# Two more up pairs of each layer, and the last single columns of gate and up, with two units in seven products

## The chip, the cores and the metric

The kernel runs on one core of one Trainium2 chip, in one launch. The metric is the time of one execution on the device in microseconds (us). A core has a TensorE (PE in the profile, with its weight loads as PEld), a VectorE (DVE), a ScalarE (ACT), a GpSimd (POOL) and a SyncE (SP). SP does no arithmetic here: it issues the transfers of the weights.

## The reference, cut to what matters

Two layers over x of 256 rows and 2048 columns, all in float32. The part that the change touches is the second half of each layer, the feed-forward block, whose hidden width is 5632:

```
h2 = rms_norm(x, ffn_norm[l])
x = x + (jax.nn.silu(h2 @ w_gate[l]) * (h2 @ w_up[l])) @ w_down[l]
```

The first half of a layer (a combined input projection, windowed attention, a spatial gating unit, sigmoid gates, an output projection) runs ahead of it with the same machinery and is left as it is.

## The kernel before, in words

**Three matmuls for one.** A float32 operand is split into a high part, rounded to the format fp32r that TensorE multiplies, and a low part, the remainder. ACT makes the high part of a weight block (`high`, line 258), DVE the low part (`low`, line 266), and `three` (lines 401 to 403) adds high x high, low x high and high x low into one PSUM bank. The 256 rows of activations (`Unit.hi` and `Unit.lo`) are the stationary operand, 128 by 128 at a time; 512 columns of weights are the moving one.

**Jobs, units, parts.** A *job* multiplies all rows by two blocks of 512 weight columns. It goes through the weights' rows in *units* of 512, four units for a matrix with 2048 rows. A unit's weights come in two transfers of 1 MB, 256 rows by 1024 columns each, into one of five buffers (`N_RAW`, line 34). Half a transfer, 256 rows by 512 columns, is a *part*. A unit that is taken *whole* has four parts; each is split once by ACT and DVE and used in 12 matmuls (two blocks of 128 rows, two of 128 in depth, three matmuls), 48 for the unit.

**Seven products.** The first `m` units of a job (`Job.m`, line 106) are multiplied by a scheme with seven block products in place of eight. With weight blocks 11, 12, 21, 22 (the first digit for the depth, the second for the columns) the products are called 11, t1, t2, 21, t3, 22 and t4; t1 to t4 take sums of weight blocks, which DVE makes (`add`, line 242, one instruction for each of the four), and sums of activations, which are made once when the activations are (`combine`, line 503). A product is a part of its own with a high and a low of its own and 6 matmuls, so the unit has 42 matmuls. Two corrections of accumulators by DVE (line 440) and some copies of them by ACT (lines 435 and 437) are made once in a job, whatever `m` is.

**The order is written out by hand.** The parts of all jobs form one list. With `m` = 2 a job starts with nine products in a row, and the last five stand between whole parts of its other units:

```
    HEAD = ("11a", "t1a", "t2a", "21a", "t3a"), ("11a", "11b", "t1a", "t1b", "t2a", "t2b", "21a", "t3a", "t3b")
    TAIL = (("22a",), ("t4a",)), (("22a",), ("22b", "21b"), ("t4a",), ("t4b",))
```

`Stream.fill` (line 270) lets ACT and DVE run ahead of TensorE by at most five parts (`N_LOW`, line 37) and issues the transfers as their buffers come free (`load`, line 199); the sums are due three to seven parts ahead of the job (`SUM_AT`, line 96). Each engine then works through its own instructions in order. Work that is neither a part nor a matmul (evictions, transpositions, splits of activations) is hung on *slots*: a whole part is one slot, a product half a slot (`tick`, line 334). How late some of it comes depends on whether the *next* job has `m` = 0, 1 or 2 (`behind`, line 311): the eviction of the job's last accumulator comes 1, 1.5 or 3 slots behind its end, the transposition of a finished block 2, 3 or 7 slots (lines 40 and 315).

**The feed-forward block.** Its 11 blocks of 512 hidden columns are taken in three rounds, (0 1 2 3), (4 5 6 7) and (8 9 10). A round goes through its columns in pairs: a gate job, whose results ACT evicts with the Silu (line 1090), and an up job, whose results DVE multiplies into them (line 1096). Blocks are then transposed by DVE and 16 small transfers from POOL's queue (`gathered`, line 481) and split again (lines 589 and 592, or 510 to 525 where sums are wanted). Block 10 stands alone: one job takes its gate columns and its up columns as the pair. Two down jobs end a round, one for each half of the output's columns; a round's first block of hidden rows goes in seven products there. What follows names a job by its first block: "up 4" multiplies the up columns of blocks 4 and 5, "gate/up 10" is the single one, "down 8" is the third round's first down job. Where `m` is set:

```
            for f in fs[::2]:
                if f + 1 < NF:
                    for w, m in ((w_gate, M_FFN[0] if f else 0), (w_up, M_FFN[1] if f in UP_TWO else 1)):
                        add_job([w[l, :, f * CW:(f + 2) * CW]], m=m)
                else:
                    add_job([w[l, :, f * CW:(f + 1) * CW] for w in (w_gate, w_up)], m=M_FFN[2])
```

(lines 177 to 182). In the kernel before, the jobs of a layer's feed-forward block have in their order: gate 0 with `m` = 0, up 0 with 2, gate 2 with 2, up 2 with 2, two downs with 1; gate 4 with 2, up 4 with 1, gate 6 with 2, up 6 with 2, two downs with 1; gate 8 with 2, up 8 with 1, gate/up 10 with 1, two downs (three units each) with 1.

Of the kernel before, what the change touches and what calls it, by code (L numbers as in the profile page):

```python
# [42 lines left out]
Q_STEP = 4  # L43
LOAD_BY = (1, 2, 3, 4)
ROUNDS = ((0, 1, 2, 3), (4, 5, 6, 7), (8, 9, 10))
M_OUT, M_FFN, M_DOWN = (0, 1), (2, 2, 1), ((1, 1), (1, 1), (1, 1))
UP_TWO = (0, 2, 6)
M_Q = 0
M_GATE, M_ATT, M_SGU = (1, 1, 1, 1), (0, 0), (1, 0)
M_V, M_U = 1, 1  # L50
# [4 lines left out]
def hybrid_trunk(ctx: ExitStack, tc: tile.TileContext, x, mix_norm, w_in, q_norm, k_norm, sinks,  # L55
# [106 lines left out]
    for l in range(DEPTH):  # L162
# [13 lines left out]
        for fs, ms in zip(ROUNDS, M_DOWN):  # L176
# [4 lines that stand above are left out]
# [970 lines left out]
```

## Time and profile before

| | |
|---|---|
| median of 3 runs | 2444.57 us (2441.78 to 2444.78) |
| the profiled execution | 2442.93 us, its span 2441.2 us |
| PE, DVE, ACT, POOL busy | 99%, 83%, 59%, 19% of the span |
| granted clock of TensorE | 0.999 |

The profile is of one execution. Its busy time counts an instruction from its start to its end; neighbouring matmuls overlap in the record, so their mean duration is longer than the step from one to the next. "Idle before, releaser" says how long an engine stood still before an instruction and which instruction ended the wait. In the view of windows a row is a stretch of time: its bounds and length, then the busy time of each engine with the number of instructions, the granted clock and the share of the transfer engines' time. The windows used here begin and end with the first matmul of a job, found by counting matmuls: a job has 48 for each whole unit and 42 for each in seven products. An instruction that overlaps the edge of a window is counted in it, so that 180 matmuls read as 181.

### The profile page before, as it was taken

How to read it: one execution, taken by the hardware profiler on the slowest of the kernel's cores; microseconds unless marked ns; L12 is line 12 of the kernel's file. 1: busy time of each engine (PE TensorE's matmuls, PEld its weight loads, DVE VectorE, ACT ScalarE, POOL GpSimd, SP SyncE). 2: the span in 40 equal slices, each digit the busy share in tenths (PEclk: the TensorE clock that was granted, in tenths of full speed). 3: DMA queues.
4: the chain of work that ended last, by engine and by line, in shares of the span. 5: the costliest groups of instructions: out<-in, count | busy, mean ns of one | idle time of the engine just before them, and what ended most of it. 6: DMA issues, size and time to landing. Idle time of an engine off the chain costs nothing. (4 is left out here: it accounts for less than half of the span.)

```text
span 2441.2 us, 30915 instructions
## 1 busy us (share of the span) xinstructions
PE 2428.7 (99%) x10926; PEld 2004.8 (82%) x10926; DVE 2015.1 (83%) x2213; ACT 1441.9 (59%) x1762; POOL 474.2 (19%) x903
## 2 busy tenths in 40 slices
PE   9999999999999999999999999999999999999999
PEld 7888888888788888888888888888888888888887
DVE  7898768787988798788879977687789887988786
ACT  6565546466655666465666655554667555755563
POOL 1421300531220022002235122014402200220020
PEclk9999999999999999999999999999999999999999
DMA  8555556776586757666776555566855766585764
GB/s 311 200 194 186 176 178 224 231 260 228 177 278 205 258 190 255 228 243 207 259 253 230 189 169 192 188 200 219 291 208 210 256 218 247 175 282 192 263 202 162
DMA packets 179053, 539.20 MB, mean 221 GB/s; under 512 B 23873, under 2 KB 26545, under 8 KB 178897
## 3 DMA queue, kind: packets, MB, share of 16 engines
q1 hardware_dynamic: 150832, 508.51, 60.6%
q0 software_dynamic: 27744, 28.44, 3.8%
q8 instruction: 85, 1.39, 0.2%
q14 instruction: 72, 0.58, 0.1%
q10 hardware_dynamic: 320, 0.27, 0.0%
HBM read 492.04 MB, written 16.78 MB: 208 GB/s over the span
## 5 line engine op out<-in xcount | busy, mean ns | idle before, releaser
L266 DVE TENSOR_TENSOR wlo<-raw,whi 128x1024 fp32r<-128x1024 f32 (+1 forms) x960 | 1153.6, 1218 | 339.8 <-PE acc L402 244.7
L258 ACT ACTIVATE whi<-raw 128x1024 fp32r<-128x1024 f32 (+1 forms) x960 | 1000.9, 1057 | 658.7 <-PE acc L403 567.5
L401 PE MATMUL acc<-whi,uh 128*128 128x512 f32 x2964 | 1160.2, 391 | 1.6 <-DVE gate L1061 1.5
L402 PE MATMUL acc<-wlo,uh 128*128 128x512 f32 x2964 | 1154.2, 389 | 2.6 <-DVE wlo L266 2.6
L403 PE MATMUL acc<-whi,ul 128*128 128x512 f32 x2964 | 1153.9, 389 | 0.2 <-DVE ul L550 0.2
L491 POOL DMA_DIRECT2D tt<-blk x800 | 393.4, 499 | 1655.7 <-DVE blk L485 714.4
L401 PEld LDWEIGHTS acc<-whi,uh 128*128 128x128 f32 x2964 | 556.4, 188 | 120.3 <-issue 2.3
L402 PEld LDWEIGHTS acc<-wlo,uh 128*128 128x128 f32 x2964 | 556.6, 188 | 118.7 <-DVE wlo L266 5.2
L403 PEld LDWEIGHTS acc<-whi,ul 128*128 128x128 f32 x2964 | 556.4, 188 | 117.1 <-DVE ul L550 0.6
L401 PE MATMUL acc<-whi,sh 128*128 128x512 f32 x496 | 193.4, 390 | 0.0
L402 PE MATMUL acc<-wlo,sh 128*128 128x512 f32 x496 | 193.2, 390 | 0.2 <-DVE wlo L266 0.2
L403 PE MATMUL acc<-whi,sl 128*128 128x512 f32 x496 | 193.1, 389 | 0.0
L258 ACT ACTIVATE whi<-sum 128x1024 fp32r<-128x1024 f32 x124 | 131.2, 1058 | 103.3 <-PE acc L403 95.6
L266 DVE TENSOR_TENSOR wlo<-sum,whi 128x1024 fp32r<-128x1024 f32 x124 | 150.4, 1217 | 4.2 <-PE acc L402 4.2
L401 PEld LDWEIGHTS acc<-whi,sh 128*128 128x128 f32 x496 | 93.1, 188 | 20.6 <-ACT acc L437 1.5
L402 PEld LDWEIGHTS acc<-wlo,sh 128*128 128x128 f32 x496 | 93.1, 188 | 20.0 <-DVE wlo L266 0.9
L403 PEld LDWEIGHTS acc<-whi,sl 128*128 128x128 f32 x496 | 93.1, 188 | 19.5
L437 ACT ACTIVATE acc<-acc 128x512 f32<-128x512 f32 x144 | 84.7, 588 | 25.3 <-PE acc L403 24.9
L242 DVE TENSOR_TENSOR raw<-raw,sum 128x1024 f32<-128x1024 f32 x62 | 75.9, 1225 | 2.1
L242 DVE TENSOR_TENSOR raw<-raw,raw 128x1024 f32<-128x1024 f32 x62 | 75.6, 1219 | 1.7 <-DMA raw<-in_w_gate_dram 1.7
L242 DVE TENSOR_TENSOR sum<-raw,raw 128x1024 f32<-128x1024 f32 x62 | 75.8, 1222 | 1.2
L242 DVE TENSOR_TENSOR sum<-raw 128x1024 f32<-128x1024 f32 x62 | 75.6, 1219 | 1.2 <-DMA raw<-in_w_gate_dram 1.2
(126 smaller groups left out, 1013.5 us busy)
## 6 DMA issues: line engine op xcount, KB each, us to landing
raw<-in_w_in_dram SPq DMA_DIRECT2D x112, 1024.0 KB, 5.4
raw<-in_w_down_dram SPq DMA_DIRECT2D x88, 1024.0 KB, 6.6
raw<-in_w_gate_dram SPq DMA_DIRECT2D x80, 1024.0 KB, 6.4
raw<-in_w_up_dram SPq DMA_DIRECT2D x80, 1024.0 KB, 6.5
raw<-in_w_out_dram SPq DMA_DIRECT2D x32, 1024.0 KB, 7.1
tt<-blk POOLq DMA_DIRECT2D x800, 32.0 KB, 4.8
raw<-in_w_attn_branch_dram SPq DMA_DIRECT2D x16, 1024.0 KB, 6.1
raw<-in_w_sgu_branch_dram SPq DMA_DIRECT2D x16, 1024.0 KB, 5.5
```

The lines of the kernel that those rows point to most:

```text
L242: nc.vector.tensor_tensor(out=self.raw(dst), in0=self.raw(one), in1=self.raw(two), op=ALU.subtract)
L258: nc.scalar.activation(hi[:, k, :], raw[:, k, :], AF.Copy)
L266: nc.vector.tensor_tensor(out=lo[:, k, :], in0=raw[:, k, :], in1=hi[:, k, :].bitcast(F32), op=ALU.subtract)
L401: nc.tensor.matmul(ps, a, hi, start=first, stop=False, skip_group_check=True)
L402: nc.tensor.matmul(ps, a, lo, start=False, stop=False, skip_group_check=True)
L403: nc.tensor.matmul(ps, b, hi, start=False, stop=last, skip_group_check=True)
L437: nc.scalar.activation({"11": x, "t2": e, "t3": y}[name], a, AF.Copy)
L491: nc.gpsimd.dma_start(blocks(d)[:, :, i] if whole else d[:, i].rearrange("p k t c -> p (k t) c"), src)
```

## The change

Two constants. `UP_TWO` lists the first blocks of those up pairs that have `m` = 2 (the others have 1); `M_FFN` holds `m` for the gate pairs, the up pairs in `UP_TWO`, and the single columns.

```diff
-M_OUT, M_FFN, M_DOWN = (0, 1), (2, 2, 1), ((1, 1), (1, 1), (1, 1))
-UP_TWO = (0, 2, 6)
+M_OUT, M_FFN, M_DOWN = (0, 1), (2, 2, 2), ((1, 1), (1, 1), (1, 1))
+UP_TWO = (0, 2, 4, 6, 8)
```

So in each of the two layers up 4, up 8 and gate/up 10 take two of their four units in seven products where they took one. Through `behind`, the jobs ahead of these three (gate 4, gate 8, up 8) hang their late work on later slots. The sums of the activations that a second unit needs are made already, for the jobs that had `m` = 2 before.

## Prediction

> **What bounds the kernel now.** I read the page first, then the waits, then the windows cut at the jobs of the feed-forward block.
>
> ```profile
> span 2441.2 us, 30915 instructions
> PE 2428.7 (99%) x10926; PEld 2004.8 (82%) x10926; DVE 2015.1 (83%) x2213; ACT 1441.9 (59%) x1762; POOL 474.2 (19%) x903
> ```
> ```profile
> L258 ACT ACTIVATE whi<-raw 128x1024 fp32r<-128x1024 f32 (+1 forms) x960 | 1000.9, 1057 | 658.7 <-PE acc L403 567.5
> ```
> ```profile
> ACT whi L258 <- PE acc L403: 663.0, 512, 3.5
> DVE wlo L266 <- PE acc L402: 248.9, 232, 1.9
> PEld acc L402 <- DVE wlo L266: 6.0, 9, 1.0
> PE acc L402 <- DVE wlo L266: 2.7, 6, 0.6
> ```
>
> In the waits of the whole span, under the page's lines, ACT (663.0 us; its row of the page gives 1057 ns for a high part) and DVE (248.9 us) stand for TensorE to free a buffer; TensorE stands for DVE's low parts a few us in all. So time goes with the number of matmuls, as long as DVE keeps ahead. Whether it does is read job by job. The rows are, in the second layer, up 0, gate 2, up 2; gate 4, up 4, gate 6, up 6; gate 8, up 8, gate/up 10, down 8.
>
> ```profile
> core 0: us, PE busy (x) PEld busy (x) DVE busy (x) ACT busy (x) POOL busy (x), PEclk, DMA share, GB/s
> ...
> 1790.30:1831.10 40.80, 40.80 (x181) 33.79 (x181) 39.08 (x37) 25.45 (x27) 0.37 (x1) 1.00 0.63 232
> 1831.10:1871.90 40.80, 40.80 (x181) 33.80 (x181) 40.70 (x43) 26.73 (x30) 15.39 (x32) 1.00 0.64 232
> 1871.90:1913.60 41.70, 41.19 (x181) 33.72 (x181) 39.37 (x38) 27.43 (x30) 1.09 (x3) 1.00 0.55 202
> ...
> 1997.90:2038.70 40.80, 40.80 (x181) 33.78 (x180) 35.00 (x32) 26.12 (x28) 0.00 (x0) 1.00 0.62 232
> 2038.70:2080.90 42.20, 42.20 (x187) 34.83 (x186) 32.88 (x31) 22.69 (x25) 1.30 (x3) 1.00 0.58 200
> 2080.90:2121.70 40.80, 40.80 (x181) 33.79 (x181) 40.70 (x42) 28.77 (x31) 14.39 (x30) 1.00 0.66 232
> 2121.70:2162.70 41.00, 41.00 (x181) 33.72 (x181) 38.68 (x37) 25.91 (x28) 1.08 (x3) 1.00 0.56 205
> 2247.00:2287.80 40.80, 40.80 (x181) 33.78 (x180) 35.00 (x32) 26.13 (x28) 0.00 (x0) 1.00 0.63 232
> 2287.80:2330.00 42.20, 42.20 (x187) 34.83 (x186) 31.25 (x29) 22.69 (x25) 1.31 (x3) 1.00 0.59 200
> 2330.00:2372.20 42.20, 42.20 (x188) 34.91 (x187) 35.83 (x36) 25.70 (x28) 14.39 (x30) 1.00 0.68 223
> 2372.20:2404.40 32.20, 32.20 (x148) 26.75 (x147) 27.48 (x27) 18.54 (x21) 0.00 (x0) 1.00 0.73 245
> ```
>
> A job with `m` = 2 has 180 matmuls and takes 40.80 us where nothing is late: 40.80 / 180 = 0.2267 us a matmul, at a granted clock of 1.00. One with `m` = 1 has 186 and takes 42.20. Three rows matter most. In gate 2 and gate 6 DVE is busy 40.70 of 40.80 us, yet TensorE loses nothing. In up 2 TensorE loses 41.70 - 40.80 = 0.90 us, in up 6 only 0.20. Here is that wait at the matmul, with DVE's rows around it:
>
> ```profile
> 1881.05 0.50 PE L402 MATMUL acc<-wlo,uh 128*128 128x512 f32 x1 [0.51 <-DVE wlo L266]
> ```
> ```profile
> 1837.55 4.62 DVE L266 TENSOR_TENSOR wlo<-raw,whi 128x1024 fp32r<-128x1024 f32 x4
> ...
> 1879.77 5.76 DVE L266 TENSOR_TENSOR wlo<-raw,whi 128x1024 fp32r<-128x1024 f32 x5
> ```
> ```profile
> 2059.22 1.23 DVE L266 TENSOR_TENSOR wlo<-raw,whi 128x1024 fp32r<-128x1024 f32 x1 [1.49 <-PE acc L402]
> ```
>
> Four low parts in a row took 4.62 us and five 5.76, so a further DVE instruction over 1024 columns costs 1.14 us. The last row is up 4 before the change: DVE waits 1.49 us for TensorE at each whole part, so its five buffers are full there. That lead is what a seven-product head lives on: a product lasts 6 x 0.2267 = 1.36 us on TensorE and takes DVE 1.14 us, or 2.28 with a subtraction. The head drains the lead, the whole parts (12 x 0.2267 = 2.72 us for 1.14) restore it. Gate 2 and gate 6 also carry the transposed blocks of the up job ahead of them, so they hand on a smaller lead; up 2 then starts with too little.
>
> **The change part by part.** *Removed:* each of six jobs (up 4, up 8, gate/up 10, twice) has 48 - 42 = 6 matmuls less, 6 x 0.2267 = 1.36 us, 8.16 us in all, and all of it where TensorE sets the pace.
>
> *Added on DVE:* seven low parts and four subtractions in place of four low parts, 7 x 1.14 = 8.0 us a job. Up 4 had 32.88 of 42.20 us, up 8 had 31.25, gate/up 10 had 35.83. The sums 40.9, 39.2 and 43.8 stand against 40.80 now. The third overflows as a plain sum, but a window is not a closed account: DVE prepares up to five parts and their subtractions ahead, so work of one job sits in the window before. The nearest rows are therefore whole jobs of the same make-up. *Added on ACT:* three more high parts a job, 3 x 1.06 = 3.2 us where it is busy 22.69 to 25.70 of 42.20: nothing. *Transfers:* the same bytes in the same order; only when a buffer comes free changes.
>
> *Moved:* gate 4, gate 8 and up 8 now have an `m` = 2 job behind them. The gates' last eviction, on ACT, comes at 3 slots in place of 1.5; its bank is wanted again by the ninth product, and gate 2 ahead of up 2 does exactly that. Up 8's last eviction on DVE comes at 3 slots, and block 9's transposition, with its 16 transfers on POOL, at 7 in place of 3. Its low part is due at slot 14.5 of gate/up 10's 15 and wanted at the seventh step of down 8, some 8 us later; POOL is busy 14.39 of 42.20 us there and nothing of this job queues behind it. All this costs nothing; without that cover down 8 would wait for one split, about 1.2 us.
>
> *What the new jobs become, with both ends.* Up 4 and up 8 follow a gate in which DVE is idle for 5.8 us (35.00 of 40.80), so they start with full buffers, at least as good a start as up 0 has, whose row is 40.80: no loss, at worst up 2's 0.90. Gate 6 follows an up job with `m` = 2, as gate 2 does: 40.80 again, no loss; the other end is gate 2 of the first layer, below. Up 6 then takes up 2's place: 0.90 in place of 0.20, so 0.70 more. Gate/up 10 stands to up 8 as gate 2 to up 0: no loss. Down 8 now starts with a small lead, like up 2, but its head has five products and four subtractions where up 2's has nine and six: two subtractions less are 2.28 us of DVE, more than the 0.90 that up 2 missed. So no loss; the other end is up 2's own. The same three jobs in the first layer:
>
> ```profile
> 578.90:619.70 40.80, 40.80 (x181) 33.78 (x180) 38.02 (x36) 25.46 (x27) 0.00 (x0) 1.00 0.63 232
> 619.70:661.15 41.45, 41.16 (x182) 33.63 (x180) 41.35 (x43) 28.89 (x31) 15.75 (x32) 1.00 0.64 229
> 661.15:703.30 42.15, 41.37 (x181) 33.63 (x180) 39.83 (x38) 26.13 (x28) 1.08 (x3) 1.00 0.54 200
> ```
> ```profile
> 607.87 1.23 DVE L242 TENSOR_TENSOR raw<-raw,raw 128x1024 f32<-128x1024 f32 x1 [1.53 <-DMA raw<-in_w_gate_dram]
> ```
> ```profile
> 588.24 0.46 SPq L361 DMA_DIRECT2D kept<-x  x1
> 588.96 1.58 SPq L222 DMA_DIRECT2D raw<-in_w_up_dram  x2
> 590.59 0.71 SPq L361 DMA_DIRECT2D kept<-x  x1
> ```
>
> Gate 2 loses 0.65 us here and up 2 1.35, because DVE stood 1.53 us for a weight transfer at the end of up 0: SP had put stores of x between the loads. Such stores fall into gate 4 and gate 8 (eight slots behind the downs), not into up 4 or up 8. So I take the second layer's values.
>
> Sum for a layer: -1.36 (up 4) + 0 (gate 6) + 0.70 (up 6) - 1.36 (up 8) - 1.36 (gate/up 10) + 0 (down 8) = -3.38 us; for two, -6.8. With no wait at all it is -8.2. With every other end taken (0.90 for up 4 and for up 8, 0.65 for gate 6 and for gate/up 10, 1.35 - 0.20 = 1.15 for up 6, 1.35 for down 8) a layer would pay 5.60 for its 4.08, and the kernel lose 3.0. Against the profiled execution of 2442.93 us the sum gives 2436.1. That execution is 1.6 below the median of the three runs, which spread over 3.0 us; from their middle, 2443.3, it gives 2436.5, and that is my number.
>
> **The rivals.**
>
> *No new wait.* The lead of up 4 is better than up 0's, since no transfer is late in it, and up 6 stays at 41.00. For it: in up 0 of the second layer too DVE and ACT stood for weights, 0.8 and 1.8 us, so its followers are no clean measure:
>
> ```profile
> ACT whi L258 <- DMA raw<-in_w_gate_dram: 1.8, 1, 1.8
> ...
> DVE sum L242 <- DMA raw<-in_w_gate_dram: 0.8, 1, 0.8
> ```
>
> Against it: DVE is at 40.70 of 40.80 already in gate 6, so a smaller start is not made good there. 2443.3 - 8.2 = 2435.1. Chance 0.12.
>
> *Late transfers in the new tails.* A job with `m` = 2 keeps four of five buffers until its subtractions are made, so its loads come in bursts. If up 4 and up 8 show what up 0 of the first layer shows, a layer loses 0.65 + 1.15 + 0.65 = 2.45 of its 4.08 us: 2443.3 - 3.3 = 2440.0, and 2442.7 if down 8 stalls by its 1.35 too. For it: the row of 1.53 us. Against it: the stores that caused it are elsewhere. Chance 0.22; within 0.2%.
>
> *Slower: buffers that starve DVE.* Gate 8, up 8 and gate/up 10, and gate 4 to up 6, are now three and four jobs in a row that hold four of five weight buffers. If each converted job lost what the longest single wait for a low part's raw transfer could take, the gain is gone from 1.36 us a job, and it is slower by over 0.2% (4.9 us) from (8.2 + 4.9) / 6 = 2.2 us a job. With the 1.53 us wait of DVE twice a job, 3.1 us, it would be 2443.3 + 18.4 - 8.2 = 2453.5. For it: the bursts. Against it: three such jobs in a row (up 0 to up 2) lost 2.0 us together at most, 0.7 a job. Chance 0.05.
>
> *TensorE is not what the spacing shows.* If the step of 0.2267 us came from what feeds the matmuls and not from the matmuls, taking 36 away would gain nothing: 2443.3. Against it: ACT and DVE both wait for TensorE in the rows above, and jobs with 6 matmuls less are 1.4 us shorter. Chance 0.03. The Trainium skill, "TensorE: Matmul & The Clock Gate", section "Back-to-back issue gap", speaks for this rival: it gives about 131 ns as the sustained spacing of matmuls with 512 columns, and about 216 ns for one alone, which it calls an over-count. By the 216 the removed work would be 7.8 us, and by the 131 it would be 4.7 us (estimates from that page); the 226.7 ns over the 180 matmuls of a job here bear out neither as a sustained step.
>
> That the change does nothing is excluded by the loop that sets `m`: blocks 4 and 8 are first blocks of pairs, and block 10 is the single one.
>
> **How the numbers follow.** The forecast has 0.58. About 0.2%, 4.9 us, is what a measurement of this kernel can tell from no change. The forecast (6.8 us) and the first rival lie beyond it: 0.70 faster. The second and the fourth: 0.25 the same. The third: 0.05 slower. The range runs from the fastest run less the whole 8.2 us, 2441.8 - 8.2 = 2433.6, to the slowest run less the gain under late transfers, 2444.8 - 3.3 = 2441.5.
>
> **What would show it.** Instructions: PE 10926 - 36 = 10890, DVE 2213 + 42 = 2255 (18 low parts, 24 subtractions), ACT 1762 + 18 = 1780. In the windows up 4, up 8 and gate/up 10 read 40.8 us, gate 6 40.8, up 6 41.5 to 41.7, down 8 32.2. Wrong would be: a loss inside up 4 or up 8 themselves; gate 6 or gate/up 10 above 41; down 8 above 32.5; a wait of DVE for a weight transfer of more than 1 us in the tails of up 4 or up 8; or the same job lengths with a median that does not follow them.

## The result, and the profile after

The changed kernel takes 2436.98 us, the median of 7 runs (2434.32 to 2440.39). The kernel before takes 2443.64 in 7 runs beside it (2441.31 to 2444.78). The ratio is 0.9973 with a 95% interval of 0.9963 to 0.9982, so the gain is 6.6 us by the ratio, between 4.4 and 9.0 (6.7 between the medians). The forecast was 2436.5 us and a gain of 6.8. One execution of a later experiment (the first with the stores moved to up 2) ran all its matmuls at some 0.8 us each, 8724.4 us in span; it is left out of everything below.

The page of the changed kernel begins:

```profile
span 2435.3 us, 30948 instructions
## 1 busy us (share of the span) xinstructions
PE 2422.0 (99%) x10890; PEld 1998.4 (82%) x10890; DVE 2058.1 (85%) x2255; ACT 1457.8 (60%) x1780; POOL 475.2 (20%) x903
```

The counts are those of the prediction: 36 matmuls fewer, 42 instructions more on DVE and 18 more on ACT. DVE is busy 43 us longer, and the span is shorter. In the windows by job, second layer, the rows are up 0, gate 2, up 2; gate 4, up 4, gate 6, up 6; gate 8, up 8, gate/up 10, down 8:

```profile
1789.10:1829.90 40.80, 40.80 (x181) 33.80 (x180) 38.69 (x37) 25.32 (x27) 0.96 (x2) 1.00 0.63 232
1829.90:1870.70 40.80, 40.80 (x181) 33.80 (x180) 40.70 (x42) 26.91 (x30) 14.73 (x31) 1.00 0.65 232
1870.70:1911.80 41.10, 41.09 (x181) 33.64 (x180) 38.77 (x37) 27.23 (x30) 1.08 (x3) 1.00 0.57 205
1996.10:2036.90 40.80, 40.80 (x181) 33.80 (x180) 37.27 (x34) 26.11 (x28) 0.00 (x0) 1.00 0.63 232
2036.90:2077.70 40.80, 40.80 (x181) 33.79 (x180) 37.98 (x36) 25.77 (x28) 1.32 (x3) 1.00 0.56 207
2077.70:2118.50 40.80, 40.80 (x181) 33.80 (x180) 40.70 (x42) 28.76 (x31) 14.32 (x30) 1.00 0.64 231
2118.50:2159.50 41.00, 41.00 (x181) 33.70 (x180) 38.70 (x37) 25.90 (x28) 1.06 (x3) 1.00 0.57 206
2243.90:2284.70 40.80, 40.80 (x182) 33.78 (x181) 37.27 (x34) 26.24 (x28) 0.00 (x0) 1.00 0.62 232
2284.70:2325.50 40.80, 40.80 (x182) 33.78 (x181) 38.06 (x36) 25.77 (x28) 1.39 (x3) 1.00 0.57 207
2325.50:2366.30 40.80, 40.80 (x182) 33.78 (x181) 39.94 (x41) 27.42 (x30) 14.24 (x30) 1.00 0.68 231
2366.30:2398.50 32.20, 32.20 (x148) 26.67 (x147) 28.43 (x29) 19.31 (x23) 0.00 (x0) 1.00 0.71 245
```

Up 4, up 8 and gate/up 10 went from 42.20 to 40.80 us, and the jobs behind them lost nothing. Gate 6 is at 40.80 as before, down 8 at 32.20 as before. Up 6 is at 41.00, where the prediction had put 41.5 to 41.7. So the changed jobs gained 1.4 us each, 8.4 by these rounded windows and 8.2 by the matmuls, and this profile has no new wait in or behind them.

The span fell by 5.9 us only. The rest lies in jobs that the change does not touch. The second layer's two output jobs and gate 0 took 3.4 us more (130.3 and 133.7 us together), while gate 2 of the first layer, up 2 of the second and the kernel's first job took 1.6 us less. Here are those three jobs, first in the kernel before and then in the changed one:

```profile
1660.10:1704.70 44.60, 43.86 (x194) 35.99 (x193) 34.80 (x38) 20.22 (x20) 17.18 (x35) 1.00 0.69 215
1704.70:1746.90 42.20, 42.20 (x188) 34.96 (x187) 35.32 (x42) 30.67 (x43) 15.74 (x32) 1.00 0.80 270
1746.80:1790.30 43.50, 43.50 (x193) 36.04 (x192) 31.17 (x36) 27.32 (x38) 16.84 (x34) 1.00 0.65 223
```
```profile
1655.40:1701.20 45.80, 44.51 (x193) 35.74 (x192) 33.66 (x36) 19.99 (x20) 17.75 (x37) 1.00 0.68 210
1701.20:1743.90 42.70, 42.47 (x188) 34.85 (x187) 34.65 (x42) 30.33 (x43) 15.69 (x32) 1.00 0.75 250
1743.90:1789.10 45.20, 43.80 (x193) 35.96 (x192) 34.20 (x39) 27.31 (x38) 16.80 (x34) 1.00 0.66 230
```

### The profile page after: what moved, and what is told of

Its sections match the earlier page's. It is cut to its first block, busy times and chain, and to the rows that moved or that the text cites. A ratio compares the mean times of both kernels' runs of the same rounds, so it can differ in the third digit from the quotient of the medians.

```text
span 2435.3 us, 30948 instructions
## 1 busy us (share of the span) xinstructions
PE 2422.0 (99%) x10890; PEld 1998.4 (82%) x10890; DVE 2058.1 (85%) x2255; ACT 1457.8 (60%) x1780; POOL 475.2 (20%) x903
## 5 line engine op out<-in xcount | busy, mean ns | idle before, releaser
L401 PE MATMUL acc<-whi,uh 128*128 128x512 f32 x2904 | 1137.0, 392 | 2.9 <-DVE gate L1061 1.5
L402 PE MATMUL acc<-wlo,uh 128*128 128x512 f32 x2904 | 1130.9, 389 | 1.4 <-DVE wlo L266 1.4
L403 PE MATMUL acc<-whi,ul 128*128 128x512 f32 x2904 | 1130.8, 389 | 0.7 <-DVE ul L592 0.5
L403 PEld LDWEIGHTS acc<-whi,ul 128*128 128x128 f32 x2904 | 545.1, 188 | 115.4 <-DVE ul L592 1.4
L402 PEld LDWEIGHTS acc<-wlo,uh 128*128 128x128 f32 x2904 | 545.3, 188 | 114.9 <-DVE wlo L266 3.8
L258 ACT ACTIVATE whi<-sum 128x1024 fp32r<-128x1024 f32 x136 | 143.9, 1058 | 120.8 <-PE acc L403 98.1
L401 PE MATMUL acc<-whi,sh 128*128 128x512 f32 x544 | 212.1, 390 | 0.2 <-ACT acc L437 0.2
L402 PE MATMUL acc<-wlo,sh 128*128 128x512 f32 x544 | 212.0, 390 | 0.1
L403 PE MATMUL acc<-whi,sl 128*128 128x512 f32 x544 | 211.8, 389 | 0.0
L266 DVE TENSOR_TENSOR wlo<-sum,whi 128x1024 fp32r<-128x1024 f32 x136 | 165.2, 1219 | 10.5 <-PE acc L402 9.7
```

The lines of the kernel that those rows point to most:

```text
L258: nc.scalar.activation(hi[:, k, :], raw[:, k, :], AF.Copy)
L266: nc.vector.tensor_tensor(out=lo[:, k, :], in0=raw[:, k, :], in1=hi[:, k, :].bitcast(F32), op=ALU.subtract)
L401: nc.tensor.matmul(ps, a, hi, start=first, stop=False, skip_group_check=True)
L402: nc.tensor.matmul(ps, a, lo, start=False, stop=False, skip_group_check=True)
L403: nc.tensor.matmul(ps, b, hi, start=False, stop=last, skip_group_check=True)
```

## The experiments

Two explanations stood against each other. The *theory of the lead*: TensorE sets the pace as long as each low part is done before its product; up 4 and up 8 start with full buffers and fill them again, so each conversion is worth its 6 matmuls and nothing is lost behind it. The *prediction's step*: an up job with `m` = 2 leaves the gate job behind it a smaller lead, so up 6 loses what up 2 loses. The *lead* is the time by which DVE has finished a low part before TensorE begins the product, and the *start* of a job is its lead at the first product. A third question was why only 6.6 us of the 8.2 showed.

**Half of the change: up 4 alone.**

```diff
-M_OUT, M_FFN, M_DOWN = (0, 1), (2, 2, 1), ((1, 1), (1, 1), (1, 1))
-UP_TWO = (0, 2, 6)
+M_OUT, M_FFN, M_DOWN = (0, 1), (2, 2, 1), ((1, 1), (1, 1), (1, 1))
+UP_TWO = (0, 2, 4, 6)
```

> Only up 4 of each layer takes two units in seven products; up 8 and gate/up 10 are as before. Theory of the lead (DVE fills its five low parts again within up 4, so gate 6 starts as before): up 4 is 40.8 us in place of 42.2, gate 6 stays at 40.8 and up 6 at 41.0; the kernel is 2 x 1.36 = 2.7 us faster than the kernel before. The prediction's step (gate 6 hands on less, up 6 takes up 2's place): up 6 at 41.5 to 41.7, the kernel 1.3 us faster.

Measured: 2441.36 us against 2444.22 before, ratio 0.9986 (0.9977 to 0.9995). In the windows, second layer, up 4, gate 6, up 6:

```profile
2037.30:2078.10 40.80, 40.80 (x182) 33.78 (x180) 38.01 (x36) 25.80 (x28) 1.35 (x3) 1.00 0.55 207
2078.10:2118.90 40.80, 40.80 (x182) 33.78 (x180) 40.70 (x42) 28.78 (x31) 14.32 (x30) 1.00 0.64 231
2118.90:2159.90 41.00, 41.00 (x182) 33.71 (x180) 38.65 (x37) 25.90 (x28) 1.10 (x3) 1.00 0.56 206
```

Up 6 stays at 41.0. The prediction's step is wrong already in this half; the windows say so, not the time, whose interval holds a gain of 2.7 us and one of 1.3.

**Half of the change: the single columns alone.**

```diff
-M_OUT, M_FFN, M_DOWN = (0, 1), (2, 2, 1), ((1, 1), (1, 1), (1, 1))
+M_OUT, M_FFN, M_DOWN = (0, 1), (2, 2, 2), ((1, 1), (1, 1), (1, 1))
 UP_TWO = (0, 2, 6)
```

> Only gate/up 10 of each layer takes two units in seven products. Theory of the lead: gate/up 10 is 40.8 us in place of 42.2 and down 8 stays at 32.2 to 32.3, in both layers; the kernel is 2.7 us faster than before. Rival (down 8 starts with too small a lead, or the half-sized transfers of this job come late): down 8 at 33 or more, or gate/up 10 above 41, and less than 1.5 us gained.

Measured: 2441.58 us, ratio 0.9987 (0.9978 to 0.9996). Gate/up 10 is at 40.80 in both layers, down 8 at 32.6 in the first and 32.2 in the second. The 32.6 lies between what the theory of the lead and its rival had said. It is not the only one: in sixteen starts of down 8 behind a converted gate/up 10 with five buffers for low parts, in all eight profiles, two lost more than 0.2 us, this one and 32.8 in the second layer of the last profile of the changed kernel:

```profile
2364.50:2397.30 32.80, 32.53 (x148) 26.69 (x147) 28.46 (x29) 19.88 (x23) 0.00 (x0) 1.00 0.69 241
```

In both, ACT stood 1.6 and 1.8 us for the small transfers of a transposed block, and TensorE then stood for ACT's copy of an accumulator (0.5 and 0.7 us at its weight loads), not for DVE. Behind an unconverted gate/up 10, down 8 read 32.17 in all eight starts. So the theory of the lead holds for gate/up 10. Down 8 now starts 6.6 us ahead in place of 7.3 to 9.4, and the conversion can cost it up to 0.6 us now and then; two cases of sixteen against none of eight do not prove it.

The same execution also holds the longest up 2 of all, in the second layer, a job that this half does not change:

```profile
1871.60:1915.20 43.60, 41.46 (x181) 33.54 (x180) 40.00 (x38) 27.31 (x30) 1.04 (x3) 1.00 0.54 194
```
```profile
ACT uh L589 <- DMA tt<-blk: 5.9, 1, 5.9
...
PE acc L401 <- ACT acc L437: 2.1, 2, 1.7
```

This again is a wait for ACT, which stood for late small transfers.

**The changed kernel again.**

> The changed kernel once more, unaltered. In its first profile the second layer's two output jobs and gate 0 took 3.4 us more than in the kernel before, and that is where the jobs' 8.2 us became 6. Theory of chance (some transfer was late in that one execution): these three jobs read 44.6, 42.2 and 43.5 us here, and the times scatter by 3 to 6 us from run to run in both kernels; median gain 6 to 8.5 us. Rival (the change shifts later work so that these jobs lose): they read 45.8, 42.7 and 45.2 again.

Measured: 2436.11 us (2434.52 to 2436.31), ratio 0.9961 (0.9949 to 0.9974). The three late jobs read 45.0, 42.7 and 44.4: 132.1 us together, between the 130.3 of the first profile of before and the 133.7 of the first of after. Neither expectation held cleanly, so the kernel before was profiled twice more.

**The kernel before, twice more.**

> The kernel before, unaltered, for a second profile. If the 1 to 3.4 us more of the second layer's output jobs and gate 0, seen in the changed kernel and in both halves of the change, are chance, they can show here too (45.0 to 45.8, 42.7, 44.4 to 45.2 us); if the changed program brings them, they read 44.6, 42.2 and 43.5 as in the first profile of before.

> The kernel before, a third profile. The second layer's two output jobs and gate 0 together took 130.2 and 131.4 us in its first two profiles, and 131.8 to 133.8 in nine of kernels with the change or half of it. If that is chance, it can read above 132 here; if the changed programs bring some 2 us there, it reads 130.2 to 131.5 again.

Measured: 2447.92 and 2444.78 us in single runs; the three jobs took 131.4 and 132.1 us. Before thus has 130.3, 131.4 and 132.1 in three profiles, and the changed kernel 133.7, 132.1 and 132.2 (the last from a later run). The ranges touch, and the first profile of before was the lowest of all. What grows there are waits for the small transfers of transposed blocks. In the waits of this stretch, before (first profile) and then after:

```profile
ACT uh L589 <- DMA tt<-blk: 10.6, 2, 6.3
```
```profile
ACT uh L589 <- DMA tt<-blk: 16.8, 3, 7.9
```

So more than half of what the first pair of profiles showed there is scatter between executions: the means of the two threes differ by 1.4 us, not by 3.4. Whether the changed program adds something like a microsecond there is left open: three profiles against three cannot say. All nine profiles of kernels with the change or half of it and five buffers lie at 131.8 to 133.8, six of them above the highest of before, which speaks for such an addition without showing its cause.

**Why up 2 waits: the stores moved away from up 0.** The second output job's two stores of x come 31 slots later, in up 2:

```diff
-                    after(KEEP_LATE if nxt is not None else 7 if c == 0 else 8, lambda: keep_x(o))
+                    after(KEEP_LATE + (31 if j and scale is not None else 0) if nxt is not None else 7 if c == 0 else 8,
+                          lambda: keep_x(o))
```

> The changed kernel with the second output job's two stores of x 31 slots later, in up 2 in place of up 0. Theory (up 2 loses because stores delay the loads at the end of up 0): gate 2 at 40.8 and up 2 at 41.0 us in both layers, as gate 6 and up 6 are; the changed kernel's profile has 40.95 and 42.19, 40.80 and 41.11, so 1 to 2 us faster than it. Rival (up 2 loses because an m = 2 job with the transposed blocks hands on a small lead, stores or not): up 2 at 41.5 to 42.2 in both layers, no change.

> The changed kernel with the second output job's two stores of x 31 slots later, in up 2 in place of up 0, once more, for a profile at the usual step of 0.227 us a matmul. Theory (stores delay the loads at the end of up 0): gate 2 at 40.8 and up 2 at 41.0 us in both layers; 0.5 to 2 us faster than the changed kernel's 2436 to 2437. Rival (a small lead is handed on, stores or not): up 2 at 41.3 to 42.2 and no change.

Measured: medians 2434.99 and 2435.31 us, ratios to before 0.9959 (0.9946 to 0.9973) and 0.9963 (0.9949 to 0.9976). Gate 2 and up 2 in the second of these runs, first and second layer:

```profile
620.30:661.10 40.80, 40.80 (x181) 33.81 (x180) 40.70 (x42) 28.73 (x31) 14.62 (x30) 1.00 0.65 233
661.10:702.10 41.00, 41.00 (x182) 33.73 (x180) 38.66 (x37) 25.91 (x28) 1.35 (x3) 1.00 0.61 232
...
1829.10:1869.90 40.80, 40.80 (x182) 33.80 (x181) 40.70 (x42) 27.25 (x30) 14.56 (x30) 1.00 0.65 232
1869.90:1910.90 41.00, 41.00 (x182) 33.75 (x181) 38.62 (x38) 26.94 (x30) 1.17 (x3) 1.00 0.61 231
```

Up 2 now takes what up 6 takes, in both layers. Without the stores among the loads, an `m` = 2 job ahead of it costs it no more than up 6's 0.2 us. That the stores alone are the cause does not follow yet.

**The stores put into up 4 and up 8.** If stores alone do it, up 4 must suffer from them too. The stores behind the downs of the first two rounds were hung later:

```diff
-                    after(KEEP_LATE if nxt is not None else 7 if c == 0 else 8, lambda: keep_x(o))
+                    after(KEEP_LATE if nxt is not None else 18 if c == 0 else 19, lambda: keep_x(o))
```

> The changed kernel with the stores of x behind the first two rounds' downs eleven slots later, so that those of the second down job fall into the first half of up 4 and up 8, where up 0 has its own. Theory (late loads at the end of such an up job take the lead from the two jobs behind it): DVE waits for a weight transfer at the end of up 4 and up 8, gate 6 reads 40.8 to 41.4 and up 6 41.3 to 42.2 us, gate/up 10 40.8 to 41.4; 1 to 4 us slower than the changed kernel. Rival (up 4 refills the lead whatever its loads do, since it starts full): gate 6 40.8, up 6 41.0, no change.

Measured: 2436.51 us, ratio 0.997 (0.9958 to 0.9982); up 4, gate 6 and up 6 at 40.8, 40.8 and 41.0. But only one of the two stores fell among the loads in question; SP had issued the other before it paused for free buffers. So once more, with both on up 0's slots (`19` in place of `18 if c == 0 else 19`):

> As the run with stores in up 4, where only one of the two stores fell between the loads at the end of the head; here both are hung on the slots that up 0's stores have. Theory A (two stores among these loads are enough to empty DVE's lead): DVE waits about 1 us for a weight transfer in up 4 and up 8, gate 6 and gate/up 10 40.8 to 41.4, up 6 41.1 to 42.2 us. Theory B (up 4 starts with a full lead, 9.2 us ahead, where up 0 starts 4 to 6 us ahead, so it asks for the same loads sooner and can stand the delay): gate 6 and gate/up 10 40.8, up 6 41.0 us.

Measured: 2436.59 us, ratio 0.9972 (0.996 to 0.9983). One execution now holds both cases. SP's queue in up 0 and in up 4 of the first layer:

```profile
588.00 0.46 SPq L361 DMA_DIRECT2D kept<-x  x1
588.71 1.51 SPq L222 DMA_DIRECT2D raw<-in_w_up_dram  x2
590.27 0.60 SPq L361 DMA_DIRECT2D kept<-x  x1
593.25 1.50 SPq L222 DMA_DIRECT2D raw<-in_w_gate_dram  x2
```
```profile
835.61 0.46 SPq L361 DMA_DIRECT2D kept<-x  x1
836.33 1.57 SPq L222 DMA_DIRECT2D raw<-in_w_up_dram  x2
837.95 0.56 SPq L361 DMA_DIRECT2D kept<-x  x1
840.91 17.08 SPq L222 DMA_DIRECT2D raw<-in_w_gate_dram  x5
```

The jobs up 0, gate 2, up 2, and then up 4, gate 6, up 6, with DVE's wait for weights in up 0 (up 4 has none):

```profile
578.80:619.60 40.80, 40.80 (x181) 33.78 (x180) 38.01 (x36) 25.44 (x27) 0.00 (x0) 1.00 0.63 232
619.60:660.90 41.30, 41.16 (x181) 33.62 (x180) 41.20 (x43) 28.85 (x31) 15.70 (x32) 1.00 0.66 230
660.90:703.10 42.20, 41.46 (x181) 33.63 (x181) 39.86 (x38) 26.14 (x28) 1.10 (x3) 1.00 0.55 200
...
828.20:869.00 40.80, 40.80 (x181) 33.78 (x180) 38.11 (x36) 25.79 (x28) 0.99 (x3) 1.00 0.63 233
869.00:909.80 40.80, 40.80 (x181) 33.78 (x180) 40.70 (x42) 28.73 (x31) 14.64 (x30) 1.00 0.65 232
909.80:950.80 41.00, 41.00 (x182) 33.71 (x181) 38.66 (x37) 25.89 (x28) 1.10 (x3) 1.00 0.57 206
```
```profile
DVE raw L242 <- DMA raw<-in_w_gate_dram: 1.5, 1, 1.5
```

The same stores in the same places cost gate 2 and up 2 1.7 us and gate 6 and up 6 nothing. SP issues the next job's first load 593.25 - 578.8 = 14.5 us behind the start of up 0 and 840.91 - 828.2 = 12.7 us behind that of up 4: DVE is further on and frees the buffer sooner. SP had waited for a low part of DVE both times. Theory B holds, the simple theory of the stores falls. Up 2's wait needs both the stores and up 0's small start.

The start can be read from the timelines. In the changed kernel the low part of up 0's first product is made in the DVE row below and the product begins in the PE row:

```profile
572.38 1.22 DVE L266 TENSOR_TENSOR wlo<-raw,whi 128x1024 fp32r<-128x1024 f32 x1
```
```profile
578.79 0.39 PE L401 MATMUL acc<-whi,uh 128*128 128x512 f32 x1
```

578.79 - 573.60 = 5.2 us of lead. The same two rows for up 4:

```profile
817.48 1.22 DVE L266 TENSOR_TENSOR wlo<-raw,whi 128x1024 fp32r<-128x1024 f32 x1
```
```profile
827.86 0.39 PE L401 MATMUL acc<-whi,uh 128*128 128x512 f32 x1
```

827.86 - 818.70 = 9.2 us. Measured in this way in the changed kernel's profile, gate 6 too starts 9.2 us ahead (it started 9.6 ahead before), and gate 2 of the first layer 7.6.

All profiles with five buffers for low parts can be read in this way, and they separate the two conditions. Ten of them have the stores in up 0. Where up 0 started 4.9 to 5.7 us ahead (thirteen times), gate 2 and up 2 together lost 0.7 to 2.8 us beyond up 6's 0.2; where it started 5.9 to 8.8 ahead (seven times), 0.5 or less. In the two profiles with the stores moved away, nothing was lost in four starts, and one of these was only 5.65 ahead. This compares executions that happened to differ, but it agrees with the edits. What TensorE stood for was not always the same: for DVE's low parts in the first layer, but in the four longest up 2 of the second (1.3 to 2.7 us lost) mostly for ACT, which had stood 4.5 to 5.9 us for small transfers. Whether the stores make those late too is not shown.

**One buffer less.** `N_LOW = 5` becomes `N_LOW = 4`, so that DVE can be four low parts ahead and no more.

> The changed kernel with four buffers for low parts in place of five, so that DVE can be one part less ahead. Theory of the lead (the buffers carry the heads): the smallest lead in gate 6 and gate/up 10, 1.2 us behind five buffers, goes to about zero or below, up 6 loses 1 to 1.5 us in place of 0.2, up 2 some more too; jobs with m = 1 stay at 42.2; 3 to 12 us slower than the changed kernel. Rival (DVE's throughput alone counts, 35 to 41 of 40.8 us a job): no job changes by more than 0.2.

Measured: 2448.9 us against 2443.85 before, ratio 1.0022 (1.0013 to 1.0031): the whole gain is gone and more. Up 4, gate 6, up 6 of the second layer, then up 8 and gate/up 10:

```profile
2043.80:2084.60 40.80, 40.80 (x182) 33.81 (x181) 36.87 (x35) 26.61 (x29) 0.12 (x1) 1.00 0.55 206
2084.60:2126.80 42.20, 41.44 (x182) 33.69 (x181) 42.10 (x43) 26.98 (x30) 15.51 (x32) 1.00 0.63 225
2126.70:2168.90 42.20, 41.38 (x181) 33.65 (x181) 37.96 (x37) 26.49 (x29) 0.00 (x0) 1.00 0.56 199
2294.10:2334.90 40.80, 40.80 (x182) 33.81 (x181) 36.88 (x36) 26.61 (x29) 0.10 (x1) 1.00 0.57 207
2334.90:2377.10 42.20, 41.43 (x182) 33.66 (x181) 41.23 (x42) 25.83 (x29) 15.54 (x32) 1.00 0.65 224
```

Gate 6, up 6 and gate/up 10 lose 1.2 to 1.4 us each, and gate 2 and up 2 are as long. Gate 6 starts 6.9 us ahead in place of 9.2. Within its head the lead fell to 1.2 us at its smallest with five buffers, and it falls to nothing with four. Up 4 and up 8 lose nothing even so, and a down job of four units still takes its 42.2. (Some jobs of the layers' first half move by 0.7 to 1.6 us either way, which was not followed up.) Against the medians of the changed kernel, 2435.86 to 2436.98, the loss is 12 to 13 us, at the upper end of the expected 3 to 12 or just beyond it. DVE has the same work as with five buffers, so it is the lead that pays for the heads, and the rival falls.

**The version with moved stores beside the changed kernel.**

> The changed kernel, on the same chip as the next run, to be compared with it: 2435.5 to 2437.5 us; up 2 41.1 to 42.2 us in each layer.

> The changed kernel with the second output job's stores in up 2 in place of up 0, on the same chip as the run before: up 2 at 41.0 us in both layers, and 0.5 to 1.5 us less than that run, at the edge of what can be told apart.

Measured on one chip: 2435.86 us (2434.66 to 2438.84) and 2434.82 (2434.04 to 2436.89). Up 2 is at 41.0 in both layers of the version, as expected. All three medians of the version lie below the three of the changed kernel, by about 1 us on the same chip. Gate 2 and up 2 of both layers lose 1.5, 1.3 and 0.5 us in the three profiles of the changed kernel and nothing in the version's, so the size fits, but the ranges overlap: the version beats the kernel before clearly and the changed one only at the edge. In this profile of the changed kernel up 2 of the first layer is at 41.0 with the stores in place, below the 41.1 to 42.2 that were expected; there up 0 had happened to start with 8.8 us of lead. The two loads of the next job behind the stores took 10.4 and 13.1 us to land, as long, to 0.02 us, as in the first layer's up 0 of the run with both stores. But SP issued the first of them 12.7 us behind the start of the job, not 14.5, and nothing was lost. That fits theory B too.

## Why the prediction was right, and the step that was wrong

*What bounds the kernel.* Right: TensorE's step of 0.2267 us a matmul sets the pace. Every converted job came down to 40.80 us. By the Trainium skill, "TensorE: Matmul & The Clock Gate", section "Back-to-back issue gap", a sustained matmul of 512 columns would take about 131 ns, and the 36 removed would have been worth 4.7 us (an estimate from that figure); the converted jobs show 1.36 to 1.42 us for 6, so neither that figure nor the rival that it spoke for is borne out.

*DVE's load.* Right in the way it was argued: 8.0 us more a job looks impossible as a sum for gate/up 10 (43.8 of 40.80) and is none, since work done ahead belongs to the window before. Gate 4 went from 35.00 to 37.27 us of DVE because it now prepares more of up 4's head.

*Up 4, up 8, gate 6, gate/up 10, down 8.* Right for the first four: with the change in, they read 40.80 in every profile with five buffers. Down 8 was right in most starts, but 32.8 once in the changed kernel and 32.6 once in half of it lie above the 32.5 that the prediction had named as a sign of being wrong. The step behind it was "All this costs nothing": by the waits, the later transposition can cost 0.4 to 0.6 us when its small transfers come late, too seldom and too little to move the sum. No run tested that by an edit.

*Up 6.* Wrong. "Up 6 then takes up 2's place: 0.90 in place of 0.20, so 0.70 more" measured 0.0 in all profiles of the change with five buffers. The stand-in was badly chosen. I had seen that stores fall into up 0 and not into up 4, but used that only to take the second layer's row in place of the first's. The second layer's up 0 has the same stores and the same small start (5.1 us ahead in the profile that the row was taken from, 6.3 in the changed kernel's first). With both taken into account gate 6 starts nearly full and up 6 keeps its 0.2.

*The rivals.* "No new wait", given 0.12, is what the jobs show: 8.2 us. My argument against it, that a smaller start is not made good in gate 6, is true of a start well below 9 us: gate 2 of the second layer passed on starts of 8.8, 8.5 and 8.2 us as 5.4, 5.0 and 4.7 at up 2. But gate 6 started 9.2 ahead in place of 9.6, and up 6 started 5.5 ahead both times. Late transfers cost nothing in up 4 and up 8, not even with the stores put there on purpose. DVE did not starve: in the converted jobs and the ones behind them it never stood for a weight transfer in a profile with all of the change and five buffers. No run took a weight buffer away; the run with four buffers for low parts shows only what a lead that is too small costs, 1.4 us in gate 6.

*The total.* 6.8 forecast and 6.6 measured agree better than the working deserves, and that is luck. The forecast took 1.4 us off for up 6, which lost nothing. The jobs gained 8.2, and 1.6 of it did not show in that first comparison, for reasons outside these jobs. The three comparisons of the same two kernels gave 6.7, 8.1 and 7.4 us between medians; times alone cannot tell 6.8 from 8.2, the windows by job can.

## What to carry to other kernels

When one engine feeds another through a few buffers, read how far ahead it is at the start of each stage (the end of its work to the start of the use), not how busy it is: DVE's 40.70 us busy in gate 6's 40.80 cost nothing with 9.2 us of lead, and with one buffer less, 6.9 us ahead, the job lost 1.4. Before a row of another stage is taken as the stand-in for a new one, compare both starts and what else runs in the transfer queue. Half-changes whose traces are read job by job settle what end-to-end times that scatter by 3 us cannot.

## What had not been expected of the hardware

The next job's first two loads in up 4 took 11.6 and 13.0 us to land behind two stores of 512 KB, and 7.9 and 9.2 without them in the changed kernel. The 3.8 us between are near the 4.5 us that 1 MB more would take at the 233 GB/s of that window (an estimate from these numbers). Whether such a delay costs anything was decided by 1.8 us in the time of issue. The times of one and the same program in one comparison scattered by 1.8 to 7.1 us, and in the profiles the scatter sat in few places: the kernel's first job, the small transfers behind the output jobs, the loads around up 2, and the start of the second layer.
